# Embedding gather with positions: first indices from a second ring, and stores of a whole sequence in one DMA

## The chip, the cores and the metric

The kernel runs on 1 core of one Trainium2 chip. The metric is the device time of one execution in microseconds, over several runs. A run also lists its span, from the first to the last instruction; the time is longer by what lies outside the span: 4.6 us (177.92 against 173.3) in the profile. All runs here were at a granted clock of 1.0.

## The reference, cut to what matters

```python
batch, seq_len, vocab_size, d_model = 32, 512, 50000, 512
def reference(indices, embedding_table, position_embed):
    token_embed = embedding_table[indices]
    return (token_embed + position_embed).astype(np.float32)
```

One row is 2 KB. Gathered in are 32 x 512 rows (33.55 MB), as much is written, and 1 MB of positions is read.

## The kernel before

GpSimd issues 128 gathers of 128 rows, VectorE adds the positions in place, ScalarE issues the stores. (A ring is the queue of DMAs that one engine issues to.) A partition holds four neighbouring rows of a sequence (K = 4, half = 2), so a sequence takes four gathers and leaves in two stores of 512 KB.

```python
order = [(b, k) for h in range(2) for b in range(FIRST)
         for k in range(h * half, (h + 1) * half)]
order += [(b, k) for b in range(FIRST, B) for k in range(K)]
stores = []
for g, (b, k) in enumerate(order):
    if (b <= 1 and k < half) or b == B - 1:
        stores.append((g + 1, b, k, 1))                # one row per partition
    elif k % half == half - 1:
        stores.append((g + 1, b, k + 1 - half, half))  # two rows: a half store
...
# both from ScalarE's ring, ahead of the barrier in front of the body
for ins in (load(idx0[:, 0, :], idx_first[:, 0, :], s_first), load_pos(0)):
    tc.no_tile_sem_insts.add(ins.ins.name)
tc.close()
tc.compile()
load(idx0[:, 1:, :], idx_first[:, 1:, :], s_next)      # indices of sequences 1 to 3
for j in range(J):
    load(idx_raw[j * B : (j + 1) * B, :], idx_rows[:, j, :], s_raw)
load_pos(1)
...
nc.gpsimd.wait_ge(s_first, 16)
for g, (b, k) in enumerate(order):
    ...                                # g == half: also waits for s_next
    ins = nc.gpsimd.indirect_dma_start(...).then_inc(s_gather[g % LANES], 16)
    if g >= LANES:                     # LANES = 10
        ins._wait_ge(s_gather[g % LANES], rounds(g - LANES))
...
for adds, b, at, n in stores:          # after `adds` additions in all
    nc.scalar.dma_start(
        out=out_rows[b][:, at : at + n, :],
        in_=slots[b % SLOTS][:, at : at + n, :],
    )._wait_ge(s_add, adds).then_inc(done, 16)
```

Of the kernel before, what the change touches and what calls it, by code (L numbers as in the profile page):

```python
# [1 line left out]

# [4 lines left out]

P = 128
K = 4
SLOTS = 23  # L10
LANES = 10
FIRST = 4
Q = 32


@with_exitstack
def kernel(
    ctx: ExitStack,
    tc: tile.TileContext,
    indices: bass.AP,  # L20
    embedding_table: bass.AP,
    position_embed: bass.AP,
    out: bass.AP,
):







    nc = tc.nc
    f32 = mybir.dt.float32
    i32 = mybir.dt.int32
    add = mybir.AluOpType.add

    B, S = indices.shape
    V, D = embedding_table.shape
    assert S == P * K and B == 32
    J = P // Q  # L40
    assert B == Q, "indices are turned in squares of 32"


    idx_words = indices.bitcast(i32)
    idx_first = idx_words[0:FIRST].rearrange("b (p w) -> p b w", p=P)
    idx_rows = idx_words.rearrange("b (j w) -> b j w", j=J)
    out_rows = out.rearrange("b (p k) d -> b p k d", k=K)
    pos_rows = position_embed.rearrange("(p k) d -> p k d", k=K)
    table = embedding_table[:, :]

    def sbuf(name, shape, dtype):
        return nc.alloc_sbuf_tensor(name, shape, dtype).ap()

    idx0 = sbuf("idx0", [P, FIRST, 2 * K], i32)
    idx_raw = sbuf("idx_raw", [P, 2 * Q * K], i32)
    idx_t = sbuf("idx_t", [P, K, B], i32)
    pos_sb = sbuf("pos_sb", [P, K, D], f32)
    slots = [sbuf(f"slot{n}", [P, K, D], f32) for n in range(SLOTS)]
    pos_ps = nc.alloc_psum_tensor("pos_ps", [P, K, D], f32).ap()



    half = K // 2
# [4 lines that stand above are left out]
    for g, (b, k) in enumerate(order):  # L68
        if (b <= 1 and k < half) or b == B - 1:
            stores.append((g + 1, b, k, 1))  # L70
        elif k % half == half - 1:
            stores.append((g + 1, b, k + 1 - half, half))

    sems = []

    def sem(name):
        sems.append(nc.alloc_semaphore(name))
        return sems[-1]

    s_first, s_next, s_raw = sem("s_first"), sem("s_next"), sem("s_raw")  # L80
    s_pos = [sem(f"s_pos{h}") for h in range(2)]
    s_gather = [sem(f"s_gather{n}") for n in range(LANES)]

    reused = range(B - SLOTS)
    s_out, s_idx, s_ps = sem("s_out"), sem("s_idx"), sem("s_ps")
    s_add, s_rest, s_pool = sem("s_add"), sem("s_rest"), sem("s_pool")
    nums = [x.num for x in sems]
    assert nums == list(range(nums[0], nums[0] + len(nums)))
    early, late = range(nums[0], nums[-3]), range(nums[-3], nums[-1] + 1)

    def rounds(g):
        return 16 * (g // LANES + 1)

    def load(out, in_, done):
        return nc.scalar.dma_start(out=out, in_=in_).then_inc(done, 16)

    def load_pos(h):
        part = slice(h * half, (h + 1) * half)
        return load(pos_sb[:, part, :], pos_rows[:, part, :], s_pos[h])



    for ins in (load(idx0[:, 0, :], idx_first[:, 0, :], s_first), load_pos(0)):
        tc.no_tile_sem_insts.add(ins.ins.name)
    tc.close()
    tc.compile()


    load(idx0[:, 1:, :], idx_first[:, 1:, :], s_next)
# [7 lines that stand above are left out]
        if g == half:  # L117
            nc.gpsimd.wait_ge(s_next, 16)
        if g == FIRST * K:
            nc.gpsimd.wait_ge(s_idx, 1)  # L120
        if b == SLOTS and k == 0:
            done = sum(1 for x in stores if x[1] in reused)
            nc.gpsimd.wait_ge(s_out, 16 * done)  # L123
        if b < FIRST:
            where = idx0[:, b, 2 * k : 2 * k + 1]
        else:
            where = idx_t[:, k, b : b + 1]
        ins = nc.gpsimd.indirect_dma_start(  # L128
            out=slots[b % SLOTS][:, k, :],
            out_offset=None,  # L130
            in_=table,
            in_offset=bass.IndirectOffsetOnAxis(ap=where, axis=0),
        ).then_inc(s_gather[g % LANES], 16)
        if g >= LANES:
            ins._wait_ge(s_gather[g % LANES], rounds(g - LANES))


    for g, (b, k) in enumerate(order):
        if g == 7:
            nc.vector.transpose(  # L140
                out=idx_t[:],
                in_=idx_raw[:].rearrange("r (q k w) -> r k q w", k=K, w=2)[:, :, :, 0],
            )._wait_ge(s_raw, 16 * J).then_inc(s_idx, 1)
        if b == 0:
            nc.vector.tensor_copy(out=pos_ps[:, k, :], in_=pos_sb[:, k, :])._wait_ge(  # L145
                s_pos[k // half], 16
            ).then_inc(s_ps, 1)
            nc.vector.wait_ge(s_ps, k + 1)
        part = slots[b % SLOTS][:, k, :]
        nc.vector.tensor_tensor(  # L150
            out=part, in0=part, in1=pos_ps[:, k, :], op=add
        )._wait_ge(s_gather[g % LANES], rounds(g)).then_inc(s_add, 1)


    rest = 0
    for adds, b, at, n in stores:
        done = s_out if b in reused else s_rest
        rest += b not in reused
        nc.scalar.dma_start(
            out=out_rows[b][:, at : at + n, :],  # L160
            in_=slots[b % SLOTS][:, at : at + n, :],
        )._wait_ge(s_add, adds).then_inc(done, 16)



    nc.gpsimd.wait_ge(s_add, len(order))
    nc.gpsimd.drain()
    nc.gpsimd.dma_reset(early)
    nc.gpsimd.sem_clear(early).then_inc(s_pool, 1)
    nc.scalar.wait_ge(s_pool, 1)  # L170
    nc.scalar.wait_ge(s_rest, 16 * rest)
    nc.scalar.sem_clear(late)

# [1 line left out]
_INS = ['indices', 'embedding_table', 'position_embed']  # L175
_OUTS = [((32, 512, 512), 'float32')]


# [23 lines left out]
```

## Time and profile before

| | before |
|---|---|
| time, median of 4 runs | 179.29 us (178.99 to 179.32) |
| span of the profiled run | 173.3 us, at a time of 177.92 us, faster than those four |
| gathers | 128, one each 1.251 us from 3.13 to 162.06 us |
| plateau of the DMA rate | 419 GB/s from about 60 us on |
| packets of 2 KB, 4 KB, 4 B | 84, 159, 9 ns each |

The last row is from the trace's packet records: for each DMA packet its start, its duration, its size and its queue. A gather packet is two rows, 4 KB.

The timeline of GpSimd at its first gather (start, duration, engine, line, operation, count, and in brackets the idle time before and what ended it):

```profile
3.13 1.08 POOL L128 DMA_INDIRECT slot<-in_embedding_table_dram,idx  x1 [2.69 <-DMA idx<-in_indices_dram]
```

The bracket names the indices' landing as the releaser, but that had happened at 2.33 us. And four stretches of the run (length, VectorE busy, GpSimd busy, clock, DMA share, GB/s):

```profile
35.00:40.00 5.00, 2.75 (x4) 3.78 (x5) 1.00 1.02 409
40.00:45.00 5.00, 2.75 (x4) 3.78 (x5) 1.00 1.02 415
45.00:50.00 5.00, 2.75 (x4) 3.78 (x5) 1.00 1.01 410
50.00:55.00 5.00, 2.60 (x5) 3.78 (x5) 1.00 1.04 410
```

The rate is near its plateau already.

### The profile page before, as it was taken

What the parts mean: (1) busy time and instruction counts of PE and PEld (TensorE: products, weight loads), DVE (VectorE), ACT (ScalarE), POOL (GpSimd) and SP (SyncE); (2) the same over time, 40 slices, a digit from 0 to 9 for tenths busy, and PEclk for the clock granted to TensorE, in tenths of its full rate; (3) what the DMA queues carried; (4) which work ended last, traced back from release to release, by engine and by line L of the source; (5) the groups of instructions that cost most, each with busy time, mean ns of one, the idle gap of its engine ahead of it and who ended that gap; (6) DMA issues with size and microseconds to landing.
All of it is one profiled execution on the core that took longest, in us unless ns stands there. A gap on an engine that the chain in (4) does not pass through costs nothing.

```text
span 173.3 us, 387 instructions
## 1 busy us (share of the span) xinstructions
DVE 90.7 (52%) x133; POOL 121.4 (70%) x132
## 2 busy tenths in 40 slices
DVE  0433855545555554555555555545555555546551
POOL 2777777777777777777777777777777777777400
DMA  4899999999999999999999999999999999999997
GB/s 128 242 324 331 345 392 365 415 409 412 411 415 402 407 421 419 409 421 420 420 416 421 420 417 419 422 416 420 421 419 417 421 419 418 419 422 415 420 420 308
DMA packets 21059, 68.34 MB, mean 394 GB/s; under 512 B 3776, under 2 KB 3904, under 8 KB 21056
## 3 DMA queue, kind: packets, MB, share of 16 engines
q10 hardware_dynamic: 10816, 34.76, 49.8%
q0 software_dynamic: 10240, 33.56, 49.7%
q14 instruction: 3, 0.02, 0.0%
HBM read 34.75 MB, written 33.55 MB: 394 GB/s over the span
## 4 chain that ended last, share of the span: by engine, by line
POOL 68%; issue 23%; DMA 5%; DVE 1%; POOLq 0%
POOL slot L128 68%; DMA slot<-in_embedding_table_dram,idx_t 4%; DVE slot L150 1%; DMA idx<-in_indices_dram 1%; POOLq L123 0%
## 5 line engine op out<-in xcount | busy, mean ns | idle before, releaser
L128 POOL DMA_INDIRECT slot<-in_embedding_table_dram,idx_t x112 | 105.9, 946 | 34.1 <-issue 34.1
L150 DVE TENSOR_TENSOR slot<-slot,pos_ps 128x512 f32<-128x512 f32 x128 | 87.9, 687 | 74.9 <-issue 46.1
L128 POOL DMA_INDIRECT slot<-in_embedding_table_dram,idx x16 | 15.3, 954 | 7.3 <-issue 4.6
L145 DVE COPY pos_ps<-pos_sb 128x512 f32<-128x512 f32 x4 | 2.8, 688 | 4.6 <-DMA pos_sb<-in_position_embed_dram 4.6
L140 DVE STREAM_TRANSPOSE idx_t<-idx_raw 128x128 int32<-128x128 int32 x1 | 0.4, 399 | 0.0
L186 POOL MEMSET const-float32-0.0<- 128x1 f32 x1 | 0.1, 98 | 0.2 <-issue 0.2
L186 POOL MEMSET const-uint8-127<- 128x1 uint8 x1 | 0.1, 118 | 0.0
L186 POOL MEMSET const-bfloat16-1.0<- 128x1 bf16 x1 | 0.1, 113 | 0.0
L186 POOL MEMSET const-float32-1.0<- 128x1 f32 x1 | 0.1, 104 | 0.0
## 6 DMA issues: line engine op xcount, KB each, us to landing
out_dram<-slot ACTq DMA_DIRECT2D x60, 512.0 KB
out_dram<-slot ACTq DMA_DIRECT2D x8, 256.0 KB
slot<-in_embedding_table_dram,idx_t POOLq DMA_INDIRECT x112
pos_sb<-in_position_embed_dram ACTq DMA_DIRECT2D x2, 512.0 KB, 4.6
slot<-in_embedding_table_dram,idx POOLq DMA_INDIRECT x16
idx_raw<-in_indices_dram ACTq DMA_DIRECT2D x4, 32.0 KB
idx<-in_indices_dram ACTq DMA_DIRECT2D x1, 4.0 KB, 1.6
idx<-in_indices_dram ACTq DMA_DIRECT2D x1, 12.0 KB
```

What stands on the lines that cost most here:

```text
L128: ins = nc.gpsimd.indirect_dma_start(out=slots[b % SLOTS][:, k, :], out_offset=None, in_=table, in_offset=bass.IndirectOffsetOnAxis(ap=whe ...
L140: nc.vector.transpose(out=idx_t[:], in_=idx_raw[:].rearrange("r (q k w) -> r k q w", k=K, w=2)[:, :, :, 0],)._wait_ge(s_raw, 16 * J).then_ ...
L145: nc.vector.tensor_copy(out=pos_ps[:, k, :], in_=pos_sb[:, k, :])._wait_ge(s_pos[k // half], 16).then_inc(s_ps, 1)
L150: nc.vector.tensor_tensor(out=part, in0=part, in1=pos_ps[:, k, :], op=add)._wait_ge(s_gather[g % LANES], rounds(g)).then_inc(s_add, 1)
L186: nc = _bacc.Bacc("TRN2", target_bir_lowering=False, num_devices=1)
```

## The change

Its intent: fewer stores with fewer semaphore packets (the 16 packets of 4 B with which each DMA here reports that its data has landed), and a start in which ScalarE has one DMA less ahead of the barrier. The descriptors stay at 4 KB, so a whole store has two for each partition.

```diff
         if (b <= 1 and k < half) or b == B - 1:
             stores.append((g + 1, b, k, 1))
+        elif FIRST < b < B - 4:
+            if k == K - 1:
+                stores.append((g + 1, b, 0, K))
         elif k % half == half - 1:
             stores.append((g + 1, b, k + 1 - half, half))
...
-    def load(out, in_, done):
-        return nc.scalar.dma_start(out=out, in_=in_).then_inc(done, 16)
+    def load(out, in_, done, engine=nc.scalar):
+        return engine.dma_start(out=out, in_=in_).then_inc(done, 16)
...
-    for ins in (load(idx0[:, 0, :], idx_first[:, 0, :], s_first), load_pos(0)):
+    for ins in (
+        load(idx0[:, 0, :], idx_first[:, 0, :], s_first, engine=nc.sync),
+        load_pos(0),
+    ):
...
             in_=slots[b % SLOTS][:, at : at + n, :],
+            max_dma_last_dim=half * D * 4,
         )._wait_ge(s_add, adds).then_inc(done, 16)
```

## The prediction

> **What bounds the kernel now.** I read the page first: busy shares, the forty slices, the DMA queues.
>
> ```profile
> span 173.3 us, 387 instructions
> DVE 90.7 (52%) x133; POOL 121.4 (70%) x132
> DMA  4899999999999999999999999999999999999997
> GB/s 128 242 324 331 345 392 365 415 409 412 411 415 402 407 421 419 409 421 420 420 416 421 420 417 419 422 416 420 421 419 417 421 419 418 419 422 415 420 420 308
> DMA packets 21059, 68.34 MB, mean 394 GB/s; under 512 B 3776, under 2 KB 3904, under 8 KB 21056
> q10 hardware_dynamic: 10816, 34.76, 49.8%
> q0 software_dynamic: 10240, 33.56, 49.7%
> ```
>
> The DMA row is full from slice 3 to the end, and the rate climbs to a plateau near 419 GB/s. 68.34 MB / 419 GB/s = 163.1 us, so the span is those bytes plus some 10 us lost at both ends. Both queues move half each.
>
> Next, the groups by line, the chain of waits and the stretches.
>
> ```profile
> L128 POOL DMA_INDIRECT slot<-in_embedding_table_dram,idx_t x112 | 105.9, 946 | 34.1 <-issue 34.1
> L150 DVE TENSOR_TENSOR slot<-slot,pos_ps 128x512 f32<-128x512 f32 x128 | 87.9, 687 | 74.9 <-issue 46.1
> POOL 68%; issue 23%; DMA 5%; DVE 1%; POOLq 0%
> 100.00:120.00 20.00, 10.84 (x16) 15.12 (x17) 1.00 1.03 419
> 160.00:165.00 5.00, 2.91 (x5) 2.40 (x3) 1.00 1.03 419
> 165.00:170.00 5.00, 2.56 (x5) 0.00 (x0) 1.00 1.03 417
> ```
>
> In the stretches the columns are the length, VectorE busy, GpSimd busy, clock, DMA share and GB/s. The chain names GpSimd: a gather takes 946 ns and the next starts about 0.30 us after it ends, waiting for nothing shown. In the timeline the first starts at 3.13 and the last at 162.06, so 158.93 / 127 = 1.251 us each. One gather is 256 KB and brings 256 KB of stores with it: 524288 B / 1.251 us = 419 GB/s, the very plateau. So two limits coincide: GpSimd's pace, and the DMA engines. That the engines are full too I take from the packet records: between 40 and 160 us at least 16 packets are open 99% of the time, and after the last gather is issued (163.0 us) the rate stays at 417 to 419 GB/s although GpSimd has stopped. From gather to add the delay is flat, 7.3 to 7.6 us from about 33 us on: a constant backlog, mean 0.95 MB in each queue between 60 and 160 us (bytes issued less bytes moved), total never under 1.5 MB.
>
> The end is bytes: from 163.0 to 172.8 us, when the last packet ends, some 3.8 MB are still moved (the sum of rate times length over that stretch); at 419 GB/s that is 9.1 of those 9.8 us.
>
> **What the Trainium skill says.** "DMA: Bandwidth & Descriptors", section "Issuing engines are not separate DMA queues": DMAs from the scalar, sync and gpsimd engines run on the same 16 DMA engines and interleave; issuing from several only saves sequencer time. So a second ring can save the 0.41 us between ScalarE's first two issues, no bandwidth. No trace yet has a SyncE DMA. The same page, "Queues, rings and completion order": each engine round-robins between the queue rows at packet granularity; the equal shares above agree. The same page, "Why a DMA increments its semaphore by 16 and not by 1": each engine used posts one increment for a DMA. The trace agrees: 68 stores x (128 data + 16) = 9792 of q10's 10816 packets, and the loads fill the other 1024. Its section "Measured" advises at least 1 MiB per DMA for 75% of peak; here 512 KB stores, kept queued, already run in a 419 GB/s stream, so that advice has nothing left to give.
>
> **Part 1, whole stores.** Sequences 5 to 27 are 23; each gives up one store of its two. This removes 23 ScalarE issues (338 ns each, on a sequencer that has 2.5 us for each: off the path) and 23 x 16 = 368 semaphore packets of 4 B. A 4 B packet is recorded at 9 ns: 368 x 9 / 16 = 0.21 us of each engine. In the plateau recorded durations overlap by 3% (share 1.03), so 0.20 us. As the engines are full up to the end, this comes off the end: **-0.2 us**. Data packets do not change: 4096 B before and after, 159 ns each. Neither do additions, gathers, or the last four sequences.
>
> What moves: the first half of each such sequence is stored two gathers later (2.5 us), so up to 0.52 MB is withheld. Just before an issue the total backlog would fall from 1.5 to about 1.0 MB, and the store queue's own minimum, 0.63 MB now, to some 0.1 MB. That is thin for stores, but 0.9 MB of gathers stay queued, and an engine with nothing in one queue takes from the other. I count **0**, with a risk of up to +1 us from unevenness among engines. Slots cannot bind: sequence 23 asks for the stores of 0 to 8, and its first gather (g = 92) is issued near 118 us while those stores are all done by 61 us.
>
> **Part 2, first indices from SyncE.** SyncE and ScalarE are both released from the opening barrier at 0.66 us; ScalarE issues the indices at 0.737, so SyncE can do so no earlier than about 0.73. The indices then land as before, at 2.33 us. The position load is issued about 0.41 us sooner (1.15 to 0.74), ScalarE's drain and the barrier before the body (GpSimd takes it at 1.83) end about 0.4 us sooner, and so do ScalarE's other loads. But the first addition waits for the first gather (6.81 us), not for positions (4.62 us). The first gather starts at 3.13, that is 0.80 after the indices landed and 0.88 after GpSimd passed the last barrier at 2.25. If the 0.8 us follow the landing, which I think more likely (6 in 10), the gathers start as before; if they follow the barrier, up to 0.4 us sooner, and the whole train with them. Against that, the 128 packets of 32 B (1.73 to 1.99 us) now share the engines with 4 KB position packets. Those were first seen 1.09 us after their issue, so they will start near 1.8, and an index packet may stand behind one or two at 159 ns or more: +0 to +0.3 us. Mean of all this: **-0.1 us**. Earlier loads of positions and remaining indices clear a little of the traffic in front of the first gathers and stores, some **-0.1 us**.
>
> Sum: -0.2 + 0 - 0.1 - 0.1 = -0.4 us, so 179.27 - 0.4 = **178.9 us**, rounded down to 178.8 since the size of the barrier's part is the least certain and points down.
>
> **Rivals.**
> (a) The start counts in full: the gather train starts 0.4 us sooner and the DMA stream with it. For it: 0.88 us after the barrier explains the start as well as 0.80 after the landing. Time 178.4.
> (b) The position packets come first on the engines: 8 per engine x 159 ns = 1.3 us in front of the index packets, interleaved. For it: both issues fall within 10 ns. Against: position packets took 0.1 us longer from issue to first packet. Time about 180.2.
> (c) Lumpy 1 MB stores starve: engines idle at times, or gathers wait behind a store burst. The backlog of 1.0 MB speaks against idling, the store queue's 0.1 MB for it. Time 179.5 to 180.5. GpSimd wouldn't slow down, as a gather waits for the tenth before it, 12.5 us back, while landing takes under 7.5 us.
> (d) Writing 8 KB in a row for each partition eases the memory. Against: store packets already sit at 159 ns with almost no excess. The excess is in the gather packets, mean 190 ns from 10 to 30 us, falling to 159 by 80 us: over the whole run 1358.2 - 8192 x 0.159 = 55.7 us, or 3.5 us per engine, of which I count about 0.5 us after the first whole store. Time 178.3 at best.
> (e) GpSimd alone is the bound and the queue is only a follower. Then less DMA work shortens just the backlog behind the last gather, again 0.2 us.
>
> **Range and chances.** A gain of 2% is 3.6 us. GpSimd's train of 127 x 1.251 us is untouched, its start can move 0.4 us, the semaphores give 0.2 and (d) 0.5: all together 1.1 us. So faster by 2% needs something I don't see: 3%. Slower by 2% needs (b) and (c) together and more: 3%. The runs before span 0.33 us. Range: 179.27 - 1.4 to 179.27 + 0.5, that is 177.9 to 179.8; it leaves out the whole of (b) and most of (c).
>
> **What would show it.** In the profile after: 21059 - 368 = 20691 packets and 3408 under 512 B; 45 stores in all (68 - 23); 4 KB data packets at 159 ns still; 1.25 us from gather to gather; a plateau at 419 GB/s. The first gather at 3.13 us confirms the landing as its releaser, 2.7 us rival (a), over 3.5 us rival (b). Additions should still lag their gathers by about 7 us, with a saw-tooth of 5 us in it from the 1 MB stores. Wrong would be: slices of the DMA row below 9 in the plateau (c), or a rate above 425 GB/s there (d, or a DMA limit that sits higher than I read).

## The result, and the profile after

The changed kernel took 179.22 us (median of 4 runs, 179.03 to 179.66), the kernel before 179.29 us (4 runs). The ratio is 1.0004, 95% interval 0.9982 to 1.0025: the same. A ratio is the mean time of one kernel's runs over that of the other's of the same rounds, so not quite the ratio of the medians. In five rounds (e5 below) it was 1.0048, interval 1.0007 to 1.0088. So the change gains nothing, and more likely costs some tenths of a per cent.

The page of the changed kernel (span; busy; DMA by slices; rates; packets; queues; chain; groups; issues):

```profile
span 175.0 us, 364 instructions
DVE 90.2 (52%) x133; POOL 121.4 (69%) x132
DMA  4889999999999999999999999999999999999996
GB/s 139 278 239 388 324 367 409 367 401 387 370 405 413 419 411 418 420 420 420 420 419 420 420 420 420 420 420 420 420 420 420 419 420 420 420 420 419 420 417 238
DMA packets 20690, 68.33 MB, mean 391 GB/s; under 512 B 3408, under 2 KB 3536, under 8 KB 20688
q0 software_dynamic: 10240, 33.56, 50.0%
q10 hardware_dynamic: 10304, 34.75, 49.0%
q1 hardware_dynamic: 144, 0.00, 0.0%
...
POOL 64%; issue 24%; DMA 6%; DVE 3%
...
L134 POOL DMA_INDIRECT slot<-in_embedding_table_dram,idx_t x112 | 105.9, 946 | 34.1 <-issue 34.1
L156 DVE TENSOR_TENSOR slot<-slot,pos_ps 128x512 f32<-128x512 f32 x128 | 87.3, 687 | 77.4 <-issue 52.0
...
out_dram<-slot ACTq DMA_DIRECT2D x23, 1024.0 KB
...
idx<-in_indices_dram SPq DMA_DIRECT2D x1, 4.0 KB, 2.1
```

The arithmetic of the change came out: 23 stores of 1 MB, 368 packets under 512 B fewer, and a new queue, q1, with the 144 packets of the first indices. The span is 1.7 us longer, but that overstates it. The profile of before fell on that kernel's fastest run, the one after on its slowest (179.66 us); the four spans of the changed kernel are 174.1, 174.2, 174.7 and 175.0 us. Where the page helps is the slices: in both kernels they reach the plateau, but 367, 387 and 370 GB/s stand in slices 8, 10 and 11 here, where before had 415, 412 and 411. The DMA row shows 9 in all of these. The stretches show the same:

```profile
35.00:40.00 5.00, 2.77 (x5) 3.78 (x5) 1.00 1.01 399
40.00:45.00 5.00, 3.58 (x6) 3.78 (x5) 1.00 1.00 396
45.00:50.00 5.00, 2.37 (x4) 3.78 (x5) 1.00 1.01 375
50.00:55.00 5.00, 2.06 (x3) 3.78 (x5) 1.00 1.02 401
...
100.00:120.00 20.00, 10.73 (x16) 15.13 (x17) 1.00 1.03 419
160.00:165.00 5.00, 2.74 (x4) 2.36 (x3) 1.00 1.03 419
165.00:170.00 5.00, 2.43 (x5) 0.00 (x0) 1.00 1.03 420
```

From 35 to 55 us the rate is 9 to 35 GB/s under that of before in each stretch: (10 + 19 + 35 + 9) x 5 us = 0.37 MB not moved, 0.9 us at 419 GB/s. The engines count as busy all along, because a packet that stalls (one of 4 KB that takes longer than its usual 159 ns) is a busy packet. From 100 us on the rate does not differ. By the packet records 20.90 MB had moved by 60 us, against 21.36 before. Not all of that is the whole stores' doing. The first half store that the change withholds was issued at 37.1 us in the kernel before, so slice 8, which ends at 35 us, comes too early for it, and 0.21 of the 0.46 MB were missing at 37 us already. From 37 to 70 us the changed kernel moved 13.31 MB, the kernel before 13.59. What is missing by then is hardly made up (from 70 to 160 us 37.77 MB against 37.68), and the last packet ends at 174.5 instead of 172.8 us. The delay from a gather to its addition is 8.0 to 8.5 us on the plateau instead of 7.3 to 7.6, but it is no measure of the loss: in e1 below, whose time does not change, it is 7.8 to 8.3 us.

The start, in GpSimd's timeline:

```profile
3.12 1.08 POOL L134 DMA_INDIRECT slot<-in_embedding_table_dram,idx  x1 [2.67 <-DMA idx<-in_indices_dram]
```

It is where it was, though the indices landed at 2.85 us, 0.52 us later than before (the issue list has 2.1 us from issue to landing, before 1.6), and GpSimd passed the last barrier at 1.79 instead of 2.25 us.

### The profile page after: what moved, and what is told of

It is laid out like the page before. It is cut to its first block, busy times and chain, and to the rows that moved or that the text cites. A ratio compares the mean times of both kernels' runs of the same rounds, so it can differ in the third digit from the quotient of the medians. Undisturbed runs are those within 1.5% of the kernel's fastest.

```text
span 175.0 us, 364 instructions
## 1 busy us (share of the span) xinstructions
DVE 90.2 (52%) x133; POOL 121.4 (69%) x132
## 3 DMA queue, kind: packets, MB, share of 16 engines
q0 software_dynamic: 10240, 33.56, 50.0%
## 4 chain that ended last, share of the span: by engine, by line
POOL 64%; issue 24%; DMA 6%; DVE 3%
POOL slot L134 64%; DMA slot<-in_embedding_table_dram,idx_t 5%; DVE slot L156 3%; DMA idx<-in_indices_dram 1%
```

## The experiments

Twelve kernels ran, on three chips, in five rounds, each with the kernel before beside it. As the part outside the span varies, the table also has the difference of the mean spans (six runs of each kernel against the eleven of before; plus or minus is a 95% interval worked out from their scatter). "MB by 60 us" is from the packet records of the one profiled run, 21.36 in the kernel before. "First gather" is its start in that profile.

| run | what | ratio of times | span, us | MB by 60 us | first gather, us |
|---|---|---|---|---|---|
| e1 | ring alone | 0.9990 | -0.11 +/- 0.36 | 21.38 | 2.94 |
| e2 | whole stores alone | 1.0047 | +0.81 +/- 0.35 | 21.12 | 3.13 |
| e3 | changed, positions behind the barrier | 1.0043 | +0.76 +/- 0.41 | 21.06 | 2.67 |
| e4 | 216 small packets more on each engine | 1.0107 | +1.47 +/- 0.35 | 21.23 | 3.13 |
| e5 | changed kernel again | 1.0048 | +0.95 +/- 0.45 | 21.08 | 3.37 |
| e6 | whole stores for 12 to 27 | 1.0014 | +0.47 +/- 0.48 | 21.31 | 3.13 |
| e7 | whole stores for 5 to 7 | 1.0031 | +0.55 +/- 0.54 | 21.14 | 3.13 |
| e8 | ring alone, table touched early | 1.0066 | +0.95 +/- 0.68 | 20.96 | 3.98 |
| e9 | halves, stored as late as wholes | 1.0067 | +1.16 +/- 0.41 | 21.00 | 3.13 |
| e10 | before without 2 MB of stores | 0.9998 | -0.22 +/- 0.49 | 21.43 | 3.13 |
| e11 | ring, start rearranged | 1.0010 | +0.19 +/- 0.32 | 21.33 | 2.68 |
| e12 | changed, 8 KB descriptors | 1.0055 | +0.83 +/- 0.42 | 20.80 | 3.36 |

All gave the right result but e10. The theory at the outset: the engines are full, the removed semaphore packets are worth 0.2 us, and the second ring moves next to nothing. The rival: the bursts of 1 MB cost something that cancels the gain.

### e1: the ring alone

```diff
--- before
-    for ins in (load(idx0[:, 0, :], idx_first[:, 0, :], s_first), load_pos(0)):
+    for ins in (load(idx0[:, 0, :], idx_first[:, 0, :], s_first, engine=nc.sync),
+                load_pos(0)):
```

> The kernel before, with only the first indices moved to the SyncE ring (stores stay in halves). Two theories for the start of the first gather, which was at 3.13 us before and at 3.12 after although the indices landed at 2.33 before and at 2.85 after. Theory 1, two waits: the gather starts at the later of (last barrier seen by GpSimd + 0.88 us) and (landing of the indices + 0.27 us); before, the barrier (2.25) set it, after, the landing did, as the index packets now lie among those of the positions. It expects here the landing between 2.6 and 3.0 us and the first gather 0.25 to 0.35 us behind it, so 2.9 to 3.3. Theory 2, a fixed time: something else holds the first gather at 3.1 us whatever lands; it expects 3.10 to 3.14 even if the landing is elsewhere. Time: both expect no change, ratio 0.997 to 1.003. If the longer span of the changed kernel's profile (175.0 against 173.3) were the ring's doing, the span would be 174.5 to 175.5 here and the time 0.5% longer.

Ratio 0.9990 (0.9965 to 1.0016). The indices landed at 2.67 and the first gather started at 2.94, 0.27 us behind: theory 1, and the fixed time is out. The train of gathers ran 0.15 to 0.20 us ahead, and the span followed by -0.11 us, which its interval does not tell from zero. The longer span of the changed kernel is not the ring's doing.

### e2: the whole stores alone

```diff
--- before
+        elif FIRST < b < B - 4:
+            if k == K - 1:
+                stores.append((g + 1, b, 0, K))
...
+            max_dma_last_dim=half * D * 4,
```

> The kernel before, with only the whole stores of sequences 5 to 27. The semaphore theory (engines full, 368 packets of 9 ns less): 20691 packets, time lower by 0.2 us, ratio 0.999, inside the noise. The rival, bursts of 1 MB cost something (gathers landed 8.0 to 8.5 us behind their issue in the changed kernel's profile, against 7.3 to 7.6 before): the delay from gather to addition again 8.0 to 8.5 us from 60 to 160 us, and the time up by 0.5 to 1 us, ratio 1.003 to 1.006. If the delay is that long but the time stays, the burst only moves work between the two queues. The gather packets' excess over 159 ns, which was 3.5 us per engine before and 4.9 after in one profile each, should be anywhere from 3 to 5.5: if it is chance, e1 and e2 scatter alike; if the bursts make it, e2 has over 4.5 and e1 under 4.

Ratio 1.0047 (1.0022 to 1.0072): the part that was to save 0.2 us costs 0.8. The stretches of this kernel:

```profile
35.00:40.00 5.00, 2.82 (x5) 3.78 (x5) 1.00 1.02 397
40.00:45.00 5.00, 3.26 (x5) 3.78 (x5) 1.00 1.04 412
45.00:50.00 5.00, 2.15 (x4) 3.78 (x5) 1.00 1.01 392
50.00:55.00 5.00, 2.75 (x4) 3.78 (x5) 1.00 1.00 383
```

Against before the stretches lack 12, 3, 18 and 27 GB/s (the first of them begins before any half store is withheld). The delay on the plateau was 7.1 to 7.8 us, not the 8.0 to 8.5 expected of the bursts; it grew to 8.4 only at the end. The gather packets' time over 159 ns was 3.73 us per engine, e1's 4.00, so that total is no sign of the bursts, and the test by it failed. Between 35 and 60 us alone, for all 4 KB packets, it is 0.94 here and 0.43 before.

### e3: positions behind the barrier

```diff
--- changed
     for ins in (load(idx0[:, 0, :], idx_first[:, 0, :], s_first, engine=nc.sync),
-                load_pos(0)):
+                ):
...
+    load_pos(0)
     load(idx0[:, 1:, :], idx_first[:, 1:, :], s_next)
```

> The changed kernel, with the load of the first positions issued behind the barrier, so that the first indices have the engines for themselves. Theory 1 (two waits): indices land at 2.3 us again, the barrier ends at 1.8 as in the changed kernel, so the first gather starts at 2.6 to 2.7 us, the whole train of gathers with it 0.45 us sooner, and as the DMA stream fills that much sooner the time falls by 0.3 to 0.5 us, ratio 0.997 to 0.998. Theory 2 (a fixed time): first gather at 3.1 us, ratio 0.999 to 1.001. The positions land near 5 us, still before the first gather, so they should not hold the first addition.

The first gather started at 2.67 us, as theory 1 had it. In all fourteen profiles the later of (barrier + 0.88) and (landing + 0.27) gives the start to 0.01 us. But the gain did not last: the indices of sequences 1 to 3 now landed at 5.51 us, the third gather waited for them until 5.77 (before: 5.76), and the train was back on its old times. The time, ratio 1.0043, is that of e2.

### e4: 216 small packets more on each engine

```diff
--- before
         )._wait_ge(s_add, adds).then_inc(done, 16)
+        if n == half and b >= FIRST:
+            for _ in range(2):
+                nc.scalar.dma_start(
+                    out=tiny[:, 8 * tinies : 8 * tinies + 8],
+                    in_=idx_words[0:16, 8 * tinies : 8 * tinies + 8],
+                ).then_inc(s_tiny, 16)
+                tinies += 1
...
+    nc.gpsimd.wait_ge(s_tiny, 16 * tinies)
```

> The kernel before, with two tiny loads on ScalarE's ring behind each of the 54 half stores of sequences 4 to 30: 108 DMAs of 16 descriptors of 32 B, each engine getting 108 data packets and 108 semaphore packets, 9 ns each: 1.94 us of every engine. Theory A, the engines are full up to the end and a small packet costs its recorded time: 3456 packets more (24515) and the time longer by 1.6 to 2.2 us, ratio 1.009 to 1.012. Theory B, GpSimd's pace is the bound and the engines have slack between gathers that small packets can use: ratio 0.998 to 1.003. Theory C, a semaphore packet also holds up its queue until earlier writes are done, so that its price is well above 9 ns: over 3 us longer.

Ratio 1.0107 (1.0081 to 1.0132), so 0.0107 x 174.9 = 1.9 us; the span grew by 1.47 +/- 0.35, and the rest lies outside it. That is theory A in the main: on the plateau the engines have no room. A small packet costs 9 ns by the measured time, 5 to 8 ns by the span (1.47 +/- 0.35 us over 216 packets), and no more. The stretch from 100 us shows the rate give way:

```profile
100.00:120.00 20.00, 10.97 (x17) 15.13 (x17) 1.00 1.03 416
```

With this price the 368 packets that the change removes are worth 0.1 to 0.2 us, about what the prediction gave them, so e2's loss comes from elsewhere and is about 1 us.

### e5: the changed kernel again

No edit.

> The changed kernel itself, in five rounds on one chip with the kernel before, as its first four runs left 0.25% open either way. From the parts measured apart (ring alone 0.999, whole stores alone 1.0047) the sum is 1.0037: 0.6 us longer. If the two parts don't add, anything from 1.000 to 1.005. First gather at 3.1 us or earlier, bytes moved by 60 us between 20.9 and 21.2 MB (21.36 before).

Ratio 1.0048, span +0.95 us: e1 and e2 add up within the scatter. The first gather was at 3.37 us and the landing at 3.10 (3.12 and 2.85 in the first profile of this kernel): how the index packets fall among those of the positions varies from run to run. The rate of this profile sags a second time, to 387 and 371 GB/s in slices 15 and 16 (61 to 70 us), after the store queue had fallen to 0.1 MB once more at 56.5 us.

### e6 and e7: where the loss arises

```diff
--- before (e6)                      --- before (e7)
+        elif 12 <= b < B - 4:       +        elif FIRST < b < 8:
+            if k == K - 1:          +            if k == K - 1:
+                (whole store)       +                (whole store)
```

> The kernel before, with whole stores only for sequences 12 to 27 (16 instead of 23), so that the switch comes near 70 us. Theory X, the loss is at the switch: when whole stores begin near 37 us half a megabyte is withheld while gather packets still stall, the store queue falls to 0.1 MB, stalls of gather packets are no longer covered by store packets, and 0.2 to 0.4 MB are not moved between 35 and 50 us. By 70 us nothing stalls, so nothing is lost: bytes moved by 60 us as before (21.3 to 21.4 MB), 256 semaphore packets less, time -0.14 us, ratio 0.998 to 1.001. Theory Y, every whole store costs something: 16/23 of +0.47%, ratio 1.003. Theory Z, the loss is at the end, where whole stores turn into halves again and the last gather lands 8.4 us behind its issue instead of 7.5: ratio 1.004 to 1.005 as with all 23.

> The kernel before, with whole stores only for sequences 5, 6 and 7. Theory X (loss at the switch, while gathers stall): the same loss as with 23, bytes moved by 60 us 20.9 to 21.2 MB, ratio 1.003 to 1.005. Theory Y (per store): 3/23 of 0.47%, ratio 1.0006. Theory Z (at the end): ratio 0.999 to 1.001 and the last gather's delay under 7.9 us.

e7: three whole stores instead of 23 cost +0.55 +/- 0.54 us of span; a fee per store would be 0.1, and a loss at the end of the stream 0. By the packet records its rate falls to 249 and 253 GB/s at 45 to 47 us, after the second whole store was issued at 43.3 us. e6: moved by 60 us were 21.31 MB, as if unchanged, so its whole stores lose nothing before they begin; but theory X expected nothing to be lost later either, and there it fell. Its rates drop to 359 and 307 GB/s at 81 to 83 us, after its second whole store was issued at 79.9 us, at a time when the kernel before had no stalls any more: 4 KB packets took 0.59 us per engine over their 159 ns between 76 and 100 us, in the kernel before 0.00. Its span is +0.47 +/- 0.48. The stretches with these dips, of e7, of e6 and of the kernel before (whose stretch from 45 to 50 us is above, with 410):

```profile
45.00:50.00 5.00, 2.06 (x3) 3.78 (x5) 1.00 0.98 343
80.00:85.00 5.00, 2.51 (x4) 3.78 (x5) 1.00 1.02 383
80.00:85.00 5.00, 2.70 (x4) 3.78 (x5) 1.00 1.03 419
```

So in the traces the loss comes with the going over from half to whole stores, wherever that is, and the stalls are not bound to the start of the run. The times alone would not decide this: both ratios (1.0014 and 1.0031) have 1 in their intervals. The fourteen profiles taken together do: from 37 to 70 us the seven whose half stores leave on time all that while (before, e1, e4, e6, e8, e10, e11) moved 13.52 to 13.65 MB, the seven with whole or late stores 13.02 to 13.43 MB. From 70 to 100 us, when e6 goes over, it moved 12.24 MB, the kernel before 12.54.

### e8: is it the first touch of the table?

The buffer of the load and the wait for it at the end are left out here.

```diff
--- e1
+    touched = embedding_table.bitcast(i32).rearrange("(p n s) d -> p n s d", p=16, s=25)
+    load(warm[:], touched[:, :, 0, 0:8], s_warm, engine=nc.sync)
```

> The kernel of e1 (halves, first indices from SyncE) with one more load on SyncE behind the barrier: 32 B of every 25th row of the table, 2000 descriptors, 125 on each engine, over a table of 102 MB. Every profile so far has 4 to 5 us per engine of packet time over the usual 159 ns for 4 KB, nearly all in gather packets and fading by 60 us, as if each first touch of a stretch of the table cost something. Theory P, first touch: the load takes these touches while the engines are still half idle (2.5 to 2.9 us idle in the first 5 us); the excess falls to under 2 us per engine, and the time by 0.5 to 2 us, ratio 0.988 to 0.997, the touches themselves being 2000 packets that stall. Theory Q, the excess belongs to the time since the start or to gathers as such: the excess stays at 4 to 5 us, and the time grows by some 0.1 us for the packets, up to 1 us if they delay the first gathers. Packets: 21060 + 2016 = 23076.

A miss. The stalls were as in every run: 1.68, 1.04, 0.50 and 0.23 us per engine in the first four lots of eight gathers, against 1.87, 0.97, 0.22 and 0.11 before. At this spacing of 51 KB an early touch does not help; a finer one was not tried. The first indices landed only at 3.70 us, the train started 0.85 us late, and the span grew by 0.95. That the load held the indices up is not shown: its own packets begin at 3.9 us.

### e9: form or time of the stores

```diff
--- before
-            stores.append((g + 1, b, k + 1 - half, half))
+            adds = g + 1 + half if FIRST < b < B - 4 and k < half else g + 1
+            stores.append((adds, b, k + 1 - half, half))
```

> The kernel before, where the first half store of sequences 5 to 27 waits, like a whole store, for the sequence's last addition; the stores themselves stay 512 KB of 4 KB descriptors, none is removed, the ring stays ScalarE's. Theory W (withheld bytes): what costs is that up to 0.52 MB reaches the queue 2.5 us later, so that the store queue runs dry while the next store is still on its way to the engines; then the same 0.2 to 0.4 MB are lost between 35 and 55 us, no semaphore packets are saved, span 0.7 to 1.3 us longer, ratio 1.004 to 1.007. Theory F (form): the 1 MB transfer of two descriptors for each partition is slow to reach the engines and that is what costs; then ratio 0.999 to 1.002 here and 21.3 MB or more moved by 60 us.

The stores keep their size, number and descriptors, and only the first half of each sequence leaves two gathers later. Ratio 1.0067 (1.0042 to 1.0092), span +1.16 us: the whole cost of e2, and more by about what the semaphore packets are worth (0.35 us, not resolved). Theory W holds as far as the withheld bytes go; the form of the DMA is not needed to explain the cost. One rival stays untested: in e9, as with whole stores, the two halves of a sequence leave together, so the bytes are both late and bunched. A run with late stores at even distances was not made.

```profile
35.00:40.00 5.00, 2.63 (x4) 3.78 (x5) 1.00 1.02 397
40.00:45.00 5.00, 3.75 (x7) 3.78 (x5) 1.00 1.03 398
45.00:50.00 5.00, 1.62 (x3) 3.78 (x5) 1.00 0.98 364
50.00:55.00 5.00, 2.76 (x5) 3.78 (x5) 1.00 1.03 402
```

The sag is that of the changed kernel. How the queue runs dry shows best in e7's packet records: at 40.0 us, 0.3 us after ScalarE began to issue the first whole store, 0.02 MB of the earlier stores are left; the new store's packets appear at 41.5 us and in numbers from 42 us. For about two microseconds the gathers are alone or nearly so, at 371 and 344 GB/s.

### e10: less to move

```diff
--- before
     for adds, b, at, n in stores:
+        if b in (12, 13):
+            continue
```

> The kernel before without the stores of sequences 12 and 13, wrong on purpose: 2.1 MB less, which at 419 GB/s is 5.0 us of the engines. Theory B (bytes alone set the end): span 3 to 5 us shorter, as far as GpSimd's train allows: its last gather starts at 162.1, and landing, addition and last store need some 8 us without a backlog, so at least 170 us, 3.5 us less. Theory E (equilibrium): the stalls of gather packets belong to a low backlog, not to the time since the start; so when the missing stores let the backlog fall below 1.5 MB near 70 us, stalls come back, and the backlog grows again to 1.9 MB by the end; then the span is only 0 to 1.5 us shorter, the delay from gather to addition dips below 6.5 us near 75 us and climbs back to 7 or more by 160 us, and there is packet time above 159 ns between 65 and 100 us (0.02 us per engine in the kernel before). Between them: delay stays low, no stalls: 3.5 us shorter.

The kernel moved 2.1 MB less, 5.0 us of the plateau, and ended no sooner: ratio 0.9998 (0.9973 to 1.0022), span -0.22 +/- 0.49. The stretches of this kernel:

```profile
70.00:75.00 5.00, 2.85 (x5) 3.77 (x5) 1.00 1.03 420
75.00:80.00 5.00, 3.91 (x7) 3.78 (x5) 1.00 0.94 352
80.00:85.00 5.00, 1.83 (x3) 3.78 (x5) 1.00 0.90 314
85.00:90.00 5.00, 3.02 (x5) 3.78 (x5) 1.00 0.98 340
90.00:95.00 5.00, 2.33 (x4) 3.78 (x5) 1.00 1.02 366
95.00:100.00 5.00, 2.06 (x3) 3.78 (x5) 1.00 1.00 368
100.00:105.00 5.00, 3.08 (x5) 3.78 (x5) 1.00 1.02 418
```

When the stores fail to come, the gathers' backlog drains too; for the gathers issued near 77 us the delay to the addition is 3.6 us. Stores are issued again from 79.9 us on, yet from 80 to 100 us the rate is only 314 to 368 GB/s. Stalls are back (2.84 us per engine over the 159 ns from 75 to 100 us, and 1.2 us of idle engines), until the delay is 6.4 to 7.1 us again. This is theory E: after the backlog was drained the stream of this kernel ran below 419 GB/s until it had grown back.

### e11: a start for both

```diff
--- e1
-    for ins in (load(idx0[:, 0, :], ..., s_first, engine=nc.sync), load_pos(0)):
+    for ins in (load(idx0[:, 0, :], ..., s_first, engine=nc.sync),):
...
+    load_pos(0)      # behind the barrier, now also from SyncE
```

> A candidate to beat both: stores in halves as before; first indices alone on SyncE ahead of the barrier; behind it SyncE issues the first positions and ScalarE the other first indices, so that neither waits for the other. From e3: first gather at 2.67 us; here the third gather should not wait for its indices, so the train runs 0.45 us ahead of before all along (gather 8 at 12.8 us instead of 13.26). If the train sets the end, the span falls by 0.4 to 0.5 us, ratio 0.997 to 0.998. If the bytes alone set it, and more stalls eat what the start gave, 0 to 0.2 us.

A miss. The first gather did start at 2.68 us, but the positions on the other ring shared the engines with the indices of sequences 1 to 3, which landed at 5.41 us (before 4.73; but 5.31 in e4, whose start is that of before, so the cause is argued). The third gather started at 5.67 and the ninth at 13.18, 0.08 us ahead of before. The time is that of before (1.0010, 0.9989 to 1.0031). No kernel beats the kernel before beyond the scatter.

### e12: 8 KB descriptors

```diff
--- changed
-            max_dma_last_dim=half * D * 4,
+            max_dma_last_dim=K * D * 4,
```

> The changed kernel with 8 KB descriptors in the whole stores, one for each partition. Packets of 2 KB took 84 ns and of 4 KB 159: 75 ns per 2 KB and 9 ns per packet. So an 8 KB packet should take about 309 ns, 9 ns less than two: 23 x 128 x 9 / 16 = 1.66 us less of each engine. Theory A (engine time counts in full): span 1 to 1.6 us shorter than the changed kernel's, so 0.2 to 0.8 us shorter than before, ratio 0.995 to 0.999. Theory R (turns): the engines take turns by packet, so a store burst gets two thirds of an engine; gathers wait for it and the store queue is dry for longer; the loss at the switch grows, span 0.5 to 2 us longer than before, ratio 1.003 to 1.011, and the delay from gather to addition swings by over 1 us within five microseconds.

A packet of 8 KB took 309 ns, as worked out, and from 100 to 160 us 62.92 - 37.63 = 25.29 MB moved, in the kernel before 63.22 - 38.08 = 25.14 MB: the plateau is 0.6% higher. But 20.80 MB by 60 us is the lowest of all, and the delay swung between 6.2 and 8.9 us. Ratio 1.0055 (1.0031 to 1.0079): theory R at its lower end, no better than the changed kernel. As it is no worse either (e5), it does not show that the engines take turns by packet. It does show that a dry store queue alone does not make gathers stall: from 62 us on that queue ran dry ten times for 1.3 to 1.8 us, and the gathers alone then moved 391 to 418 GB/s, their packets taking 159 to 168 ns in the mean.

## Why the prediction was right or wrong, point by point

The time was predicted at 178.8 us in a range of 177.9 to 179.8, and measured at 179.22; that it would be neither 2% faster nor 2% slower held. Luck had a part in the range: with the ratio of e5 the changed kernel would have taken 1.0048 x 179.29 = 180.2 us, above it. Three of its steps did not hold: that the end is bytes, that withholding costs nothing, and what releases the first gather.

**What bounds the kernel.** That GpSimd's pace and the DMA engines meet at 419 GB/s was right: packets added on the plateau cost most or all of their recorded time (e4), and in e8, where the train starts 0.85 us late, the span is 0.95 +/- 0.68 us longer (with 2016 packets more, so this only agrees). "The end is bytes" was wrong as it stood. e10 took away 5 us of bytes and the end stayed. The end is GpSimd's last gather plus the backlog that stands behind it then; bytes count as far as they change that backlog. In before, the changed kernel, e2, e4, e9 and e10 the last gather starts at 162.0 to 162.2 us, and the last packet ends at anything from 172.4 (e10) to 174.6 us (e9). Two of its readings were off. The delay from gather to addition was 6.8 to 7.6 us from 33 us on, not 7.3 to 7.6. And equal shares of the two queues do not test that engines take turns: they follow from equal bytes (33.56 and 34.76 MB).

**Part 1, the semaphore packets, -0.2 us.** The count (368) was right, and the price (9 ns; by e4 5 to 9) nearly so. The 0.2 us itself is under what the runs resolve.

**Part 1, "I count 0, with a risk of up to +1 us".** This is the step that failed, and with it rival (c) was set too low. The reasoning was that an engine with an empty store queue takes gathers instead. It does, and late in e12 gathers alone nearly kept the rate; but in e7, at the going over, they ran at 344 to 371 GB/s and stalled, and in the changed kernel the rate fell by 9 to 35 GB/s between 35 and 55 us. The cost is +0.8 us for the whole stores (e2) against -0.2 expected, and e9 shows that it lies in the half megabyte that comes late, not in the form of the transfer. The estimate of the store queue's minimum, 0.1 MB, was right at the going over (0.09 MB in the changed kernel, 0.11 in e2); on the plateau it is 0.35 to 0.5 MB and costs nothing. So the loss is mostly paid once, while the backlog grows to what the coarser stores need (in e5 it was paid in two sags); that is read from the traces, and e7 supports it.

**The sign named for rival (c)**, slices of the DMA row below 9 in the plateau, did not appear. The rate fell while the share stood at 1.00 to 1.02. The row of GB/s was the one to name.

**Part 2, the start.** "If the 0.8 us follow the landing, which I think more likely" was wrong: the gather follows a landing by 0.27 us and the barrier by 0.88. Rival (a) had the right wait, but the indices landed at 2.67 to 3.10 us with the positions among them, 0.34 to 0.77 us later than before, where +0 to +0.3 was expected (ahead of the positions, or without them, they landed at 2.32 to 2.62 us in the nine profiles that have that). Both errors nearly cancel in the first gather, 3.12 us. That is the very sign by which the prediction would have held its wrong reading confirmed (3.13 us); only the landing at 2.85 us gave it away. The sum, -0.1 us, agrees with e1's -0.11 +/- 0.36 and is not shown by it. The other -0.1 us, for earlier loads, no run shows.

**Rivals (b), (d), (e).** (b) did not happen in full: the index packets lay among those of the positions but not behind all of them. For (d) there is no sign: store packets sit at 159 ns, and the plateau gained under 1 GB/s. (e) is nearer to the truth than it was given credit for.

**What stays open.** Why a gather packet stalls when the backlog is low is not settled. A first touch of the table at 51 KB steps is out as the cause (e8), and so is time since the start (e6, e10); lack of store packets beside them is not enough (e12). No run tells whether it is depth of queue, something in the memory, or something else. In the first four runs the changed kernel's cost was not seen; the two intervals, 0.9982 to 1.0025 and 1.0007 to 1.0088, overlap only between 1.0007 and 1.0025.

## What to carry to other kernels

Before you merge transfers to save packets, ask what the merging withholds, and what is queued in its place until the larger transfer reaches the engines (in e7 some 2 us after its issue). In this kernel, where a steady producer and full DMA engines meet, time was lost where the backlog was thin, and taking work away in the middle (e10) brought nothing. Judge such a stream by GB/s, not by its busy share, and compare mean spans of several runs, since two single profiles differed here by 1.7 us, about twice the effect (0.95 us in e5).

## What the Trainium skill lacked or had wrong

- "DMA: Bandwidth & Descriptors", section "Rules for kernel authors", asks for at least 1 MiB per DMA for the most bandwidth. In this stream of two queues, going from 512 KB to 1 MB lengthened the span by 0.81 +/- 0.35 us (e2), and storing as late without merging did so as well (e9). The page does not speak of withheld bytes.
- The same page, section "Issuing engines are not separate DMA queues", is right that rings share the engines (index packets lay among those of the positions in e1), and lacks what follows for a small urgent load: 4 KB of indices landed at 2.33 to 2.62 us in front of the positions on one ring, and at 2.67 to 3.10 us beside them on two (3.70 in e8, which has one more load).
- No page has the time of an indirect DMA's issue on GpSimd: 128 rows took 946 ns, one each 1.251 us, and the first started 0.88 us behind a barrier or 0.27 us behind the landing of its indices, whichever was later.
- No page has packet times for these sizes (the DMA page has one figure per packet, for a 4 KB transfer of 64 packets): 9, 84, 159 and 309 ns for 4 B, 2 KB, 4 KB and 8 KB, without stalls.
